# One output tensor, a re-ordered head with nine extra matrix products, and two moves behind the w_out projection, in a streaming hybrid trunk on one core

## The chip, the core and the metric

The kernel runs on one core of a Trainium2 chip. The time is device microseconds (us) of one launch, from its first to its last instruction on the chip with a little around it. Engines are named as in the profile: PE is TensorE's matrix product, PEld its weight load, DVE is VectorE, ACT ScalarE, POOL GpSimd, SP SyncE, which issues most of the DMAs. A "q" behind a name (SPq) is the engine's instruction queue.

## The reference

One layer is computed for 256 new frames (the prompt) and 32 further frames of a running stream (the sample). Both use the same weights, so the kernel treats them as 288 tokens; only histories and states differ. All data are float32, the model width is 2048.

```python
xn   = rmsnorm(x, norm_mix_pre)
proj = xn @ w_in          # -> u_pool 1024 | z 2048 | xBC 2560 | dt 32
y_pool = pool_mixer(u_pool) ; y_ssd, new_h = ssd_mixer(z, xBC, dt, h0)
x    = x + rmsnorm(concat[y_pool, y_ssd] @ w_out, norm_mix_post)
hn   = rmsnorm(x, norm_ffn_pre)
up   = causal_dwconv(hn @ w_up)        # 2 x 5632 columns: gate, value
x    = x + rmsnorm((silu(gate) * value) @ w_down, norm_ffn_post)
# in ssd_mixer, per head:  h_last = decay * h0 + B^T (decay * dt * x)
```

Returned are x for both groups, the last rows of each convolution and pooling input, and the new states `h_last` of prompt and sample.

## The kernel before

**Products.** Activations lie transposed: 128 features on the partitions, 288 tokens along the free axis, so a width of 2048 is 16 K tiles. A float32 product is made of three products of reduced form: weight and activation are each split into a rounded high part (an ACT Copy to `whi`, or to half 0 of `xn`, `hn`, `fa`) and the remainder (a DVE subtraction to `wlo`, or to half 1). `mm3` (L135 to L138) issues high·high (L136), high·low (L137) and low·high (L138) into one PSUM accumulator. So each K tile of weights costs ACT one copy and DVE one subtraction before PE can use it.

**What sets the order.** The code is written against a framework that computes, while the program is built, in which order each engine takes its instructions, from a model of how long each lasts and from priorities. `tc.high_priority(offset=...)` moves instructions ahead, `tc.issue_after(i)` puts an instruction behind `i` on the same engine (nothing waits for it across engines), `tc.keep_in_program_order` fixes an instruction's place. On the chip each engine runs its queue in that fixed order and waits on semaphores. Buffers come from pools and are re-used in turn: five PSUM banks for accumulators (`acc_ps`), three more (`aux`), four each for raw weights, `whi` and `wlo`.

**Stages that the change touches.** The *head* (L245 to L280) computes the first 768 columns of `w_in`: 16 K tiles `k`, six accumulators, 18 products for each `k`. For each `k` it splits `xn` (`split_from`, L99 on ACT and L100 on DVE), splits the weights (L270, L271), and squares the input (`input_squares`, ACT at L233, added on POOL at L234 through two buffers `xsq`); `input_rstd` makes one product `prs` with a constant matrix `mean` (all 1/2048), which sums over partitions, and takes the root. The products `pdt` (L289) follow the head.

The *mixer* (convolution, scan, gates) and the w_out projection come next. At the projection's end lies the *turn* (L744 to L807): `mix_out` squares the last two column tiles into `msq` (L668); the products `psum_m` (L745) close their sum; `state_s` and `state_p` (L689 to L715) form the last two state groups `j` = 3, 2 of four for sample and prompt (`psts`, `pst`, six products), where POOL adds the decayed old state (L714) and SP stores it; `rm` is the root of `psum_m`. Then the residual line on DVE (`residual`, L763 and L764, and the following subtraction, chained by `in_line` in written order) makes `hn` K tile by K tile, while PE multiplies each with 896 columns of `w_up` in seven accumulators (`up1`, weights split at L798 and L799, 21 products for each `k`). Last comes the product `psum_t` (L806) with its root `r2`, written behind the second column tile of the last K tile.

The rest of the FFN is up in tiles of 256 columns and down in two halves. In the *tail* (L943 to L1054) the last two column tiles of down are finished for token block B first (`run_b`), then `y_out` (L963 to L974) scales rows of 128 tokens x 512 columns in `xr` and stores them: four stores of one prompt block, the sample's store from `xr_s` (128 partitions: 4 column blocks x 32 tokens) at L1044, four stores of the other block, after which the kernel ends.

Of the kernel before, what the change touches and what calls it, by code (L numbers as in the profile page):

```python
# [8 lines left out]
F32 = mybir.dt.float32  # L9
F32R = mybir.dt.float32r  # L10
AF = mybir.ActivationFunctionType
ALU = mybir.AluOpType
# [18 lines left out]
NF = D_FF // P  # L31
NXC = CONV // P
NU = D_POOL // P
# [10 lines left out]
def body(  # L44
# [14 lines left out]
    w_up2,  # L59
    w_up,  # L60
    w_down,
    y_prompt,
    y_sample,
    new_pool,
    new_sconv,
    new_ssd_p,
# [16 lines left out]
    def aux(shape, name):  # L83
        return aux_ps.tile(shape, F32, tag="aux", name=name)
# [7 lines left out]
    def split_from(a, src, scale=None):  # L92

        if scale is None:
            act.activation(a[:, 0, :], src, AF.Copy)
            dve.tensor_tensor(a[:, 1, :], src, a[:, 0, :].bitcast(F32), op=ALU.subtract)
        else:
            return (
                act.activation(a[:, 0, :], src, AF.Copy, scale=scale),  # L99
                dve.scalar_tensor_tensor(  # L100
                    a[:, 1, :], src, scale, a[:, 0, :].bitcast(F32), op0=ALU.mult, op1=ALU.subtract
                ),
            )
# [114 lines left out]
    start = ExitStack()  # L218
# [25 lines left out]

    act.dma_start(out=g_mix_pre, in_=g0_in)  # L245
    input_tiles(0, 1)
    first = [acc_ps.tile([P, NT], F32, tag="acc", name="acc") if m < 5 else aux([P, NT], "acc_x") for m in range(6)]
    chunks = ((0, 1), (1, 1)) + tuple((k, 2) for k in range(2, KD, 2))
    x_with = {0: (1, 1), 1: (2, 2), 2: (4, 2), 4: (6, 3), 6: (9, 3), 8: (12, 4)}
    for kb, n in chunks:  # L250
        raw = wpool.tile([P, n, 768], F32, tag="raw", name="raw")
        sp.dma_start(out=raw, in_=w_first[:, kb : kb + n, :])
        if kb in x_with:
            input_tiles(*x_with[kb])
        if kb == 1:
            pool.dma_start(out=wdt, in_=w_dt)
        if kb == 2:
            pool.dma_start(out=par1, in_=par1_in)
            pool.dma_start(out=hp, in_=hp_in)
        if kb == 6:  # L260
            pool.dma_start(out=pc, in_=par2_in[:, :120])
            pool.dma_start(out=pf, in_=par2_in[:, 120:].rearrange("p (r t) -> p r t", r=6))
        for k in range(kb, kb + n):
            a = atile("xn")
            split_from(a, xT[:, k, :], g_mix_pre[:, k : k + 1])
            xn.append(a)
            hi, lo = wtile("hi", 1, 768)[:, 0, :], wtile("lo", 1, 768)[:, 0, :]
            step = 256 if k == 0 else 768
            for c in range(0, 768, step):
                act.activation(hi[:, c : c + step], raw[:, k - kb, c : c + step], AF.Copy)  # L270
                dve.tensor_tensor(  # L271
                    lo[:, c : c + step], raw[:, k - kb, c : c + step], hi[:, c : c + step].bitcast(F32), op=ALU.subtract
                )
# [434 lines left out]
    def state_s(j, x, h, pin=False):  # L708
        st = acc_ps.tile([P, 512], F32, tag="acc", name="psts")
        ins = pe.matmul(st, btok[:, j // 2, 2, :], x[:, 2, :], start=True, stop=True)  # L710
        if pin:
            tc.keep_in_program_order(ins)
        act.activation(x[:, 2, :], st, AF.Copy)
        pool.tensor_tensor(h, h, x[:, 2, :], op=ALU.add)  # L714
        sp.dma_start(out=new_ssd_s[:, 512 * j : 512 * j + 512], in_=h)  # L715

    late_in = {}

# [8 lines left out]
    for grp in ((0, 1), (2,), (3,), (4,), (5,), (6,), (7,)):  # L727
        project(
            wov, [(256 * c, 256) for c in grp], mix, [(8, 8), (16, 8), (0, 8)],
            mix_before(grp[0]), lambda m, p_: mix_out(p_),  # L730
        )
        if 2 <= grp[0] < 4:
            x_h = state_in(grp[0] - 2)
            state_p(grp[0] - 2, *x_h)
            state_s(grp[0] - 2, *x_h)
        elif 4 <= grp[0] < 6:
            late_in[grp[0] - 2] = state_in(grp[0] - 2)
        if grp[0] == 0:
            sp.dma_start(out=xT, in_=x_in)
            act.dma_start(out=new_sconv, in_=sc_stage)  # L740
            act.dma_start(out=new_pool, in_=np_stage)


    for i in range(2):  # L744
        tc.keep_in_program_order(pe.matmul(p_m, mean, last_sq[i], start=False, stop=i == 1))  # L745
# [14 lines left out]
    def in_line(f, *args, **kw):  # L760
        with ExitStack() as order:
            if line:
                order.enter_context(tc.issue_after(line[-1].ins))  # L763
            line.append(f(*args, **kw))  # L764
        return line[-1]
# [6 lines left out]
    for k in range(KD):  # L772
        if k % 2 == 0:
            raw = wpool.tile([P, 2, 896], F32, tag="raw", name="raw")
            with tc.high_priority(offset=ahead[0]):
                sp.dma_start(out=raw, in_=w_up1[:, k : k + 2, :])
        a = atile("hn")
        hi = act.activation(a[:, 0, :], x1[k], AF.Copy, scale=g_ffn_pre[:, k : k + 1])  # L778
        if k + 1 < KD:
            residual(k + 1)  # L780
        lo = in_line(
            dve.scalar_tensor_tensor,
            a[:, 1, :], x1[k], g_ffn_pre[:, k : k + 1], a[:, 0, :].bitcast(F32), op0=ALU.mult, op1=ALU.subtract,
        )
        if k == 0:
            act.activation(xsum, x1[k], AF.Square)
        else:
            q = out_temp()
            act.activation(q, x1[k], AF.Square)
            in_line(dve.tensor_tensor, xsum, xsum, q, op=ALU.add)  # L790
        hn.append(a)
        whi, wlo = wtile("hi", 1, 896)[:, 0, :], wtile("lo", 1, 896)[:, 0, :]
        with ExitStack() as order:
            order.enter_context(tc.high_priority(offset=ahead[0]))
            if k > 3:
                order.enter_context(tc.issue_after(hi.ins))
                order.enter_context(tc.issue_after(lo.ins))
            act.activation(whi, raw[:, k % 2, :], AF.Copy)  # L798
            dve.tensor_tensor(wlo, raw[:, k % 2, :], whi.bitcast(F32), op=ALU.subtract)  # L799
        for m in range(7):  # L800
            c = slice(m * P, (m + 1) * P)
            mm3(up1[m], whi[:, c], wlo[:, c], a, k == 0, k == KD - 1)
            if k == KD - 1 and m == 1:
                r2 = const.tile([P, NT], F32, tag="spread", bufs=3, name="r2")
                with tc.high_priority(offset=1000):
                    tc.keep_in_program_order(pe.matmul(p_t, mean, xsum, start=True, stop=True))  # L806
                    root(r2, p_t)  # L807
# [155 lines left out]
    def y_out(q, b):  # L963

        x = xr[2 * q + b]
        f_ = ft[2 * q + b]
        for o, n, src in (
            ((0, 512, f_),) if q < 3 else ((0, 2 * P, f_[:, : 2 * P]), (2 * P, 2 * P, last[b]))
        ):
            c = slice(o, o + n)  # L970
            ins = dve.scalar_tensor_tensor(x[:, c], src, rf[:, b : b + 1], x[:, c], op0=ALU.mult, op1=ALU.add)  # L971
            if b:
                tc.keep_in_program_order(ins)
        sp.dma_start(out=y_prompt[0][b * P : (b + 1) * P, 512 * q : 512 * (q + 1)], in_=x)  # L974

    n_tok = [0]

# [63 lines left out]
    tc.keep_in_program_order(  # L1041
        dve.scalar_tensor_tensor(xr_s, ft_s, rf[:, 2:3], xr_s, op0=ALU.mult, op1=ALU.add)
    )
    sp.dma_start(out=y_sample[0].rearrange("s (q c) -> q s c", q=4), in_=xr_s)  # L1044
# [11 lines left out]


_OUTS = [
    (1, 256, 2048), (1, 32, 2048), (P, 2, 15, NU), (P, 2, 3, NXC), (P, D_SSD), (P, D_SSD), (P, 2, 2, 2 * NF),
]  # L1060


# [70 lines left out]
```

## Time and profile before

| | |
|---|---|
| time, three runs | 1330.11, 1330.14, 1331.14 us (median 1330.14) |
| profiled execution | 1329.91 us; its span 1328.2 us, so 1.7 us lie around the span |
| mean granted PE clock | 0.997 |
| instructions | 25077, of which PE 10041 |
| busy share of the span | PE 99%, PEld 98%, DVE 67%, ACT 50%, POOL 16% |
| HBM | 236.23 MB read, 11.95 MB written, 187 GB/s |

How to read the rows: a timeline row gives start, duration, engine, line, operation, output<-inputs with their shapes, and in brackets the idle time before it and what ended that. Products overlap in PE's pipeline: each row lasts 0.29 us, though a product starts every 0.13 us or so; the pace is read from the starts. A float32 product that is not split shows as two rows (x2). A row of a window has busy time (and count) for PE, PEld, DVE, ACT and POOL, then the granted clock, the share of the 16 DMA engines in use, and GB/s. A row of the waits view has the engine's waiting tile and line, what released it, then total us, count, longest us.

### The profile page before, as it was taken

How to read it: one execution, taken by the hardware profiler on the slowest of the kernel's cores; microseconds unless marked ns; L12 is line 12 of the kernel's file. 1: busy time of each engine (PE TensorE's matmuls, PEld its weight loads, DVE VectorE, ACT ScalarE, POOL GpSimd, SP SyncE). 2: the span in 40 equal slices, each digit the busy share in tenths (PEclk: the TensorE clock that was granted, in tenths of full speed). 3: DMA queues.
4: the chain of work that ended last, by engine and by line, in shares of the span. 5: the costliest groups of instructions: out<-in, count | busy, mean ns of one | idle time of the engine just before them, and what ended most of it. 6: DMA issues, size and time to landing. Idle time of an engine off the chain costs nothing.

```text
span 1328.2 us, 25077 instructions
## 1 busy us (share of the span) xinstructions
PE 1310.4 (99%) x10041; PEld 1295.1 (98%) x10041; DVE 884.6 (67%) x1460; ACT 666.3 (50%) x1002; POOL 215.0 (16%) x353
## 2 busy tenths in 40 slices
PE   7999999999999999999999999999999999999997
PEld 7999999999999989999999999999999999999996
DVE  8898998779644478977666643345666666664444
ACT  7558777446443455645445443334444444454442
POOL 6221102121211100211111100001111111101110
PEclk9999999999999999999999999999999999999998
DMA  7668884465666445666454454455444544566663
GB/s 287 230 194 255 287 242 160 140 240 206 232 206 207 147 143 195 199 188 185 164 183 162 151 175 161 160 180 177 172 159 164 186 159 159 175 235 175 209 181 93
DMA packets 104008, 249.81 MB, mean 188 GB/s; under 512 B 63748, under 2 KB 69444, under 8 KB 81492
## 3 DMA queue, kind: packets, MB, share of 16 engines
q1 hardware_dynamic: 101972, 243.11, 55.8%
q0 software_dynamic: 1488, 4.92, 1.1%
q8 instruction: 78, 1.28, 0.4%
q14 instruction: 38, 0.31, 0.1%
q10 hardware_dynamic: 432, 0.19, 0.1%
HBM read 236.23 MB, written 11.95 MB: 187 GB/s over the span
## 4 chain that ended last, share of the span: by engine, by line
PE 98%; DVE 1%; DMA 0%; ACT 0%; issue 0%; DVEq 0%; SPq 0%
PE acc L138 31%; PE acc L136 31%; PE acc L137 31%; PE acc_x L138 1%; PE acc_x L137 1%; PE acc_x L136 1%; PE py L467 1%; DVE xr L971 0%; PE run_a L1014 0%; PE low L1012 0%; DMA raw<-in_w_first 0%; PE py L469 0%; PE pst L701 0%; PE run_b L1027 0%; PE pdt L289 0%; DVE mg L764 0%
## 5 line engine op out<-in xcount | busy, mean ns | idle before, releaser
L131 DVE TENSOR_TENSOR wlo<-raw,whi 128x1024 fp32r<-128x1024 f32 (+1 forms) x386 | 464.0, 1203 | 334.7 <-ACT whi L130 332.5
L130 ACT ACTIVATE whi<-raw 128x1024 fp32r<-128x1024 f32 (+1 forms) x386 | 399.6, 1037 | 474.5 <-PE acc L137 382.9
L136 PE MATMUL acc<-hn,whi 128*128 128x288 f32 x1360 | 399.0, 294 | 0.1
L137 PE MATMUL acc<-hn,whi 128*128 128x288 f32 x1360 | 398.1, 293 | 0.0
L138 PE MATMUL acc<-hn,wlo 128*128 128x288 f32 x1360 | 397.7, 293 | 0.0
L136 PEld LDWEIGHTS acc<-hn,whi 128*128 128x128 f32 x1360 | 255.3, 188 | 0.9 <-ACT hn L778 0.9
L137 PEld LDWEIGHTS acc<-hn,whi 128*128 128x128 f32 x1360 | 255.3, 188 | 0.1
L138 PEld LDWEIGHTS acc<-hn,wlo 128*128 128x128 f32 x1360 | 255.2, 188 | 0.0
L136 PE MATMUL acc<-xn,whi 128*128 128x288 f32 x688 | 203.6, 297 | 5.7 <-ACT whi L270 5.7
L137 PE MATMUL acc<-xn,whi 128*128 128x288 f32 x688 | 200.6, 293 | 0.0
L138 PE MATMUL acc<-xn,wlo 128*128 128x288 f32 x688 | 198.6, 298 | 1.3 <-DVE wlo L271 1.3
L136 PE MATMUL acc<-fa,whi 128*128 128x288 f32 x660 | 194.0, 294 | 0.0
L137 PE MATMUL acc<-fa,whi 128*128 128x288 f32 x660 | 193.4, 293 | 0.0
L138 PE MATMUL acc<-fa,wlo 128*128 128x288 f32 x660 | 193.1, 293 | 0.0
L136 PEld LDWEIGHTS acc<-xn,whi 128*128 128x128 f32 x688 | 130.2, 189 | 6.6 <-ACT whi L270 5.7
L137 PEld LDWEIGHTS acc<-xn,whi 128*128 128x128 f32 x688 | 130.1, 189 | 0.2
L138 PEld LDWEIGHTS acc<-xn,wlo 128*128 128x128 f32 x688 | 127.8, 189 | 2.1 <-DVE wlo L271 1.5
L136 PEld LDWEIGHTS acc<-fa,whi 128*128 128x128 f32 x660 | 124.1, 188 | 0.0
L138 PEld LDWEIGHTS acc<-fa,wlo 128*128 128x128 f32 x660 | 123.9, 188 | 0.0
L137 PEld LDWEIGHTS acc<-fa,whi 128*128 128x128 f32 x660 | 123.9, 188 | 0.0
L825 POOL COPY fc_stage<-ebuf 128x4 f32<-128x4 f32 x88 | 27.2, 310 | 501.2 <-DVE ebuf L824 501.2
L831 DVE SCALAR_TENSOR_TENSOR fc<-ebuf,pf,fc 128x290 f32<-128x290 f32 x176 | 90.2, 518 | 2.9 <-ACT fc L829 0.3
(277 smaller groups left out, 1692.0 us busy)
## 6 DMA issues: line engine op xcount, KB each, us to landing
raw<-in_w_up SPq DMA_DIRECT2D x80, 1024.0 KB, 4.8
raw<-in_w_in SPq DMA_DIRECT2D x38, 1024.0 KB, 5.4
raw<-in_w_down SPq DMA_DIRECT2D x32, 1024.0 KB, 4.8
raw<-in_w_out SPq DMA_DIRECT2D x24, 1024.0 KB, 4.9
raw<-in_w_down SPq DMA_DIRECT2D x16, 768.0 KB, 4.3
raw<-in_w_up SPq DMA_DIRECT2D x8, 896.0 KB, 4.6
gb<-g_d SPq DMA_DIRECT2D x8, 832.0 KB, 6.4
raw<-in_w_first SPq DMA_DIRECT2D x7, 768.0 KB, 10.1
```

The source lines that it names most:

```text
L130: act.activation(hi, raw[:, k : k + n, :], AF.Copy)
L131: dve.tensor_tensor(lo, raw[:, k : k + n, :], hi.bitcast(F32), op=ALU.subtract)
L136: pe.matmul(out, wh, a[:, 0, :], start=start, stop=False)
L137: pe.matmul(out, wh, a[:, 1, :], start=False, stop=False)
L138: pe.matmul(out, wl, a[:, 0, :], start=False, stop=stop)
L467: pe.matmul(y[:, 0:256], xw[:, 0, c], m[:, j, 0:256], start=True, stop=False)
L825: pool.tensor_copy(fc_stage[:, :, :, i], e[:, 256:324].rearrange("p (s c) -> p s c", c=34)[:, :, 0:2])
L831: dve.scalar_tensor_tensor(c, e[:, r_ : r_ + 290], pf[:, r_, i : i + 1], c, op0=ALU.mult, op1=ALU.add)
```

## The change

It has four parts.

1. `y_prompt` and `y_sample` become one output `y_rows` of 128 x 9 x 512: the rows of `xr` go to places 0 to 7 of each partition, `xr_s` to place 8, and the host's reshaping puts them back. The stores of `xr` stay 128 x 512 with a longer step between rows; the store of `xr_s` changes from 4 x 32 x 512 to 128 x 512.
2. In the head, nine products `mean` x `mean` of 128 x 128, which nothing reads, stand ahead of the first real one. `xsq` gets four buffers. From `k` = 3 the split of `xn` is issued behind the split of the weights of `k` - 2, the squares behind the weight copy of `k` - 1, and `input_rstd` stands at `k` = 14 rather than 13.
3. The sample's late state addition (`j` = 3, 2) moves from POOL, where it ran right behind the copy of `psts`, to DVE, into the residual line at `k` = 4 and 5; its store on SP follows it.
4. The split of `w_up`'s K tile `k` = 3 is issued behind `hn` of `k` = 3, as that of the later tiles already was.

```diff
@@ outputs and tail
-    y_prompt,
-    y_sample,
+    y_rows,
...
-        sp.dma_start(out=y_prompt[0][b * P : (b + 1) * P, 512 * q : 512 * (q + 1)], in_=x)
+        sp.dma_start(out=y_rows[:, 4 * b + q, :], in_=x)
...
-    sp.dma_start(out=y_sample[0].rearrange("s (q c) -> q s c", q=4), in_=xr_s)
+    sp.dma_start(out=y_rows[:, 8, :], in_=xr_s)
@@ head
-            q = xin.tile([P, NT], F32, tag="xsq", bufs=2, name="xsq")
+            q = xin.tile([P, NT], F32, tag="xsq", bufs=4, name="xsq")
...
+    cut = []
+    idle = aux([P, P], "idle")
+    for i in range(9):
+        tc.keep_in_program_order(pe.matmul(idle, mean, mean, start=True, stop=True))
...
-            split_from(a, xT[:, k, :], g_mix_pre[:, k : k + 1])
+            with ExitStack() as order:
+                for ins in cut[k - 2] if k > 2 else ():
+                    order.enter_context(tc.issue_after(ins.ins))
+                split_from(a, xT[:, k, :], g_mix_pre[:, k : k + 1])
...
+            cut.append((w_hi, w_lo))
             for t in range(k - 1, k) if 0 < k < 9 else range(2 * k - 10, 2 * k - 8) if 8 < k < 13 else ():
-                input_squares(t)
-            if k == 13:
+                with tc.issue_after(cut[k - 1][0].ins):
+                    input_squares(t)
+            if k == 14:
                 input_rstd()
@@ turn
         act.activation(x[:, 2, :], st, AF.Copy)
-        pool.tensor_tensor(h, h, x[:, 2, :], op=ALU.add)
-        sp.dma_start(out=new_ssd_s[:, 512 * j : 512 * j + 512], in_=h)
+
+        def add(eng=pool):
+            ins = eng.tensor_tensor(h, h, x[:, 2, :], op=ALU.add)
+            sp.dma_start(out=new_ssd_s[:, 512 * j : 512 * j + 512], in_=h)
+            return ins
+
+        return add
...
-            state_s(grp[0] - 2, *x_h)
+            state_s(grp[0] - 2, *x_h)()
...
-    state_s(3, *late_in[3], pin=True)
-    state_s(2, *late_in[2], pin=True)
+    late_add = [state_s(j, *late_in[j], pin=True) for j in (3, 2)]
...
+        if 3 < k < 6:
+            in_line(late_add[k - 4], dve)
...
-            if k > 3:
+            if k > 2:
                 order.enter_context(tc.issue_after(hi.ins))
                 order.enter_context(tc.issue_after(lo.ins))
```

The computed order moves with it, in places that no line of the diff names. First, DVE in the head: `wlo` is the remainder of one K tile of weights, `xn` that of one K tile of the input, `g_125` the gain. Before:

```order
L271 TENSOR_TENSOR wlo<-raw,whi 128x768
L284 TENSOR_TENSOR wdt<-wdt,g_125 128x512
L271 TENSOR_TENSOR wlo<-raw,whi 128x768
L100 SCALAR_TENSOR_TENSOR xn<-xT,g_125,xn 128x288 x2
L271 TENSOR_TENSOR wlo<-raw,whi 128x768 x2
L100 SCALAR_TENSOR_TENSOR xn<-xT,g_125,xn 128x288 x6
L271 TENSOR_TENSOR wlo<-raw,whi 128x768 x2
L100 SCALAR_TENSOR_TENSOR xn<-xT,g_125,xn 128x288 x4
L271 TENSOR_TENSOR wlo<-raw,whi 128x768 x8
```

DVE in the head, the same stretch of the changed kernel:

```order
L277 TENSOR_TENSOR wlo<-raw,whi 128x768
L292 TENSOR_TENSOR wdt<-wdt,g_125 128x512
L277 TENSOR_TENSOR wlo<-raw,whi 128x768
L99 SCALAR_TENSOR_TENSOR xn<-xT,g_125,xn 128x288 x2
L277 TENSOR_TENSOR wlo<-raw,whi 128x768 x2
L99 SCALAR_TENSOR_TENSOR xn<-xT,g_125,xn 128x288 x2
L277 TENSOR_TENSOR wlo<-raw,whi 128x768 x2
L99 SCALAR_TENSOR_TENSOR xn<-xT,g_125,xn 128x288 x2
L277 TENSOR_TENSOR wlo<-raw,whi 128x768 x2
L99 SCALAR_TENSOR_TENSOR xn<-xT,g_125,xn 128x288 x2
```

Runs of six and four `xn` have become an alternation of two and two; nothing is taken out or added.

Second, ACT at the turn (the numbers behind names are those of buffers): `msq0` and `msq1` are the squares of the last two column tiles, `mg` their scaled copies, `rm` the root of `psum_m`. Before:

```order
L798 ACTIVATE whi_5887<-raw_5877 128x896
L668 ACTIVATE msq0_3581<-acc_5591 128x288
L670 ACTIVATE mg_5756<-acc_5591,par1_119 128x288
L798 ACTIVATE whi_5920<-raw_5877 128x896
L668 ACTIVATE msq1_3582<-acc_5592 128x288
L670 ACTIVATE mg_5771<-acc_5592,par1_119 128x288
L237 ACTIVATE rm_5798<-psum_m_4205,eps_t_89 128x288
```

ACT at the turn, changed:

```order
L812 ACTIVATE whi_5893<-raw_5883 128x896
L676 ACTIVATE msq0_3591<-acc_5601 128x288
L678 ACTIVATE mg_5766<-acc_5601,par1_119 128x288
L676 ACTIVATE msq1_3592<-acc_5602 128x288
L678 ACTIVATE mg_5781<-acc_5602,par1_119 128x288
L236 ACTIVATE rm_5804<-psum_m_4215,eps_t_89 128x288
```

One weight copy, that of `k` = 3, has left the place between the two squares.

Third, PE at the end of the first up tiles, around `psum_t`. Before:

```order
L136 MATMUL acc<-hn,whi 128x288
L137 MATMUL acc<-hn,whi 128x288
L138 MATMUL acc<-hn,wlo 128x288
L806 MATMUL psum_t<-xsum,mean 128x288
L136 MATMUL acc<-hn,whi 128x288
L137 MATMUL acc<-hn,whi 128x288
L138 MATMUL acc<-hn,wlo 128x288
L136 MATMUL acc_x<-hn,whi 128x288
```

PE at the same place, changed:

```order
L137 MATMUL acc<-hn,wlo 128x288 x3
L137 MATMUL acc_x<-hn,wlo 128x288 x2
L137 MATMUL acc<-hn,wlo 128x288 x2
L820 MATMUL psum_t<-xsum,mean 128x288
L135 MATMUL acc_x<-hn,whi 128x288
L136 MATMUL acc_x<-hn,whi 128x288
L137 MATMUL acc_x<-hn,wlo 128x288
```

`psum_t` has gone from 15 products ahead of the end of the last K tile to directly behind it. The next product there, into `acc_x`, belongs to the next column tile (`w_up2`), and its PSUM bank is the one that `psum_t` used.

More of the change, by code (lines that the diff above doesn't have):

```diff
@@ L269, in body @@
             for c in range(0, 768, step):
-                act.activation(hi[:, c : c + step], raw[:, k - kb, c : c + step], AF.Copy)
-                dve.tensor_tensor(
+                w_hi = act.activation(hi[:, c : c + step], raw[:, k - kb, c : c + step], AF.Copy)
+                w_lo = dve.tensor_tensor(
                     lo[:, c : c + step], raw[:, k - kb, c : c + step], hi[:, c : c + step].bitcast(F32), op=ALU.subtract
                 )
+            cut.append((w_hi, w_lo))
             for t in range(k - 1, k) if 0 < k < 9 else range(2 * k - 10, 2 * k - 8) if 8 < k < 13 else ():
-                input_squares(t)
-            if k == 13:
+                with tc.issue_after(cut[k - 1][0].ins):
+                    input_squares(t)
+            if k == 14:
                 input_rstd()
@@ L1058 @@
 _OUTS = [
-    (1, 256, 2048), (1, 32, 2048), (P, 2, 15, NU), (P, 2, 3, NXC), (P, D_SSD), (P, D_SSD), (P, 2, 2, 2 * NF),
+    (P, 9, 512), (P, 2, 15, NU), (P, 2, 3, NXC), (P, D_SSD), (P, D_SSD), (P, 2, 2, 2 * NF),
 ]
@@ L1119 @@
     r = _run(nc, [arrays], core_ids=[0])
-    y_p, y_s, n_pool, n_sconv, h_p, h_s, n_fconv = (_np.asarray(r.results[0][f"out_{i}"]) for i in range(len(_OUTS)))
+    y, n_pool, n_sconv, h_p, h_s, n_fconv = (_np.asarray(r.results[0][f"out_{i}"]) for i in range(len(_OUTS)))
     def rows(a, s):
@@ L1127, in heads @@
         return _np.ascontiguousarray(a.T).reshape(1, 1, HEADS, 64, P)
+    y_p = _np.ascontiguousarray(y[:, :8].reshape(P, 2, D_MODEL).transpose(1, 0, 2)).reshape(1, NP_, D_MODEL)
+    y_s = _np.ascontiguousarray(y[:, 8].reshape(4, NS, 512).transpose(1, 0, 2)).reshape(1, NS, D_MODEL)
     return (
```

## The prediction

> **What bounds the kernel now.** I read the busy shares first, then the view of PE's waits, then the timeline at the few places where PE waits or crawls, last the chain at the end.
>
> ```profile
> PE 1310.4 (99%) x10041; PEld 1295.1 (98%) x10041; DVE 884.6 (67%) x1460; ACT 666.3 (50%) x1002; POOL 215.0 (16%) x353
> PE acc L136 <- ACT whi L270: 5.7, 1, 5.7
> PE acc L138 <- DVE wlo L271: 1.3, 1, 1.3
> PE psum_f L931 <- ACT fsq L960: 0.8, 1, 0.8
> PE psum_m L745 <- ACT msq L668: 0.7, 1, 0.7
> ```
>
> PE is busy for 99% of the span; the change takes none of its products away and adds nine. What can be won lies where PE waits (two of the four listed waits lie in the head, one at the turn), where its products run at less than their pace, and after its last product. The stretches concerned, in order of time: the start of the head,
>
> ```profile
> 5.71 0.61 PE L136 MATMUL acc<-xn,whi 128*128 128x288 f32 x1 [5.71 <-ACT whi L270]
> 10.87 0.29 PE L137 MATMUL acc<-xn,whi 128*128 128x288 f32 x1
> 5.71:10.87 5.16, 5.16 (x22) 5.16 (x22) 3.95 (x7) 3.69 (x9) 2.49 (x5) 1.00 1.02 376
> 30.25 0.94 PE L138 MATMUL acc<-xn,wlo 128*128 128x288 f32 x5 [1.30 <-DVE wlo L271]
> 48.39 2.08 PE pdt L289 x32
> ```
>
> The row 5.71:10.87 is a window: 22 products in 5.16 us, 0.23 us for each. From 10.87 to 48.39 run the other 266 of the 288, one wait of 1.30 and `prs`; with 0.48 us for `prs` (its row is below) that is (37.52 - 1.30 - 0.48) / 266 = 0.134 us a product, little over half as much. The slow start so costs 5.16 - 22 x 0.134 = 2.2 us. The granted clock in the window's row says 1.00 in spite of it, so I go by the starts.
>
> **The head: nine products and the order.** The changed kernel's first product needs only `mean`, which POOL writes at 0.95 to 1.15. A float32 product of 128 columns, and one of 288, cost:
>
> ```profile
> 0.95 0.20 POOL L183 MEMSET mean<- 128x128 f32 x1
> 112.46 0.22 PE pcb L422 x2
> 40.81 0.48 PE prs L242 x2
> 10.42 1.58 ACT L270 ACTIVATE whi<-raw 128x768 fp32r<-128x768 f32 x2 [1.47 <-DMA raw<-in_w_first]
> 17.98 4.32 DVE L100 SCALAR_TENSOR_TENSOR xn<-xT,g,xn 128x288 fp32r<-128x288 f32 x6
> 25.19 3.53 DVE L100 SCALAR_TENSOR_TENSOR xn<-xT,g,xn 128x288 fp32r<-128x288 f32 x4
> ```
>
> At half pace 0.22 becomes 0.44, so nine last 4.0 us, from about 1.2 to 5.2: just ahead of 5.71, when the first weights are there. They cost nothing unless one takes over (5.71 - 1.2) / 9 = 0.50 us. PE has then been busy for 4.0 us by 5.2; before, full pace came after 5.16 us of work. Bounds for what they bring: nothing, or all of the 2.2. I take all of it, since 4.0 of idle work and 1.2 of real work make the 5.16 by 6.4, and what is still slow there is swallowed by a new wait: K tiles 0 and 1 (36 products, 4.8 us) end by 10.5, but `whi` of `k` = 2 starts at 10.42 behind its DMA and takes half of 1.58, until 11.2. That wait of 0.7 us comes in where PE used to arrive late, so 1.5 remain.
>
> [...]
>
> The stall of 1.30 at 30.25 goes: there `wlo` stood behind runs of six and four `xn` on DVE (4.32 and 3.53 us), which the new order breaks up into twos. ACT and POOL have the squares behind the weight copies now; `prs`, which needs their sum, stands one K tile later, so it is not hurried. Head: 1.5 + 1.3 = 2.8 us. If the idle products bring nothing, 1.3; if the order brings nothing either, 0.
>
> **The turn.**
>
> ```profile
> 475.28 0.95 ACT L798 ACTIVATE whi<-raw 128x896 fp32r<-128x896 f32 x1 [0.63 <-PE acc L137]
> 476.13 0.39 ACT L668 ACTIVATE msq<-acc 128x288 f32<-128x288 f32 x1
> 476.58 0.75 PE L745 MATMUL psum_m<-msq,mean 128*128 128x288 f32 x2 [0.72 <-ACT msq L668]
> 478.88 3.60 PE L701 MATMUL pst<-sx,btok 128*128 128x512 f32 x8
> 478.90 2.71 POOL L714 TENSOR_TENSOR sh<-sh,sx 128x512 f32<-128x512 f32 x2 [20.01 <-ACT sx L713]
> 480.52 1.41 DVE L764 TENSOR_TENSOR mg<-mg,xT 128x288 f32<-128x288 f32 x1
> 482.33 0.46 DVE L764 TENSOR_TENSOR mg<-mg,xT 128x288 f32<-128x288 f32 x1
> 482.55 0.67 PE L136 MATMUL acc<-hn,whi 128*128 128x288 f32 x3
> ```
>
> The weight copy of 0.95 stands between the last product and the last square, and PE waits 0.72 for that square. With the copy gone (its place is behind `hn` of `k` = 3) the square starts when the product is done, and the 0.72 goes nearly whole. Next late is `hn` of `k` = 0: its first addition on DVE took 1.41 us while POOL worked at its two additions, against 0.46 for the same form right after them. Without POOL's additions that is some 0.95 us earlier, while PE has its six state products to do until about 482.4 (3.60 from 478.88), so only 0.1 to 0.2 us show. I take 0.9 for both; bounds 0.6 and 1.1.
>
> **DVE in the up tiles.** DVE gets `wlo` of `k` = 3 later and two additions of 128x512. Nearest rows:
>
> ```profile
> 489.42 1.08 DVE L799 TENSOR_TENSOR wlo<-raw,whi 128x896 fp32r<-128x896 f32 x1
> 497.41 1.08 DVE L799 TENSOR_TENSOR wlo<-raw,whi 128x896 fp32r<-128x896 f32 x1
> 500.06 1.09 DVE L799 TENSOR_TENSOR wlo<-raw,whi 128x896 fp32r<-128x896 f32 x1
> 1317.85 0.74 DVE L1042 SCALAR_TENSOR_TENSOR xr_s<-ft_s,rf,xr_s 128x512 f32<-128x512 f32 x1
> ```
>
> DVE needs 2.65 us for a K tile (from 497.41 to 500.06); PE needs 21 products, 21 x 0.134 = 2.8. So DVE only just keeps pace, and 1.08 + 2 x 0.75 = 2.6 us more must come out of its lead. At 489.42 it subtracts for `k` = 4, which PE reaches four tiles behind 482.55, at about 493.7: a lead of 3 us over the end of the subtraction. `wlo` is used only in the last third of a tile, which gives 1.8 more. I count nothing; bounds 0 and 1.5. Behind the additions, their two stores go to SP between loads of raw weights; an SP issue lasts 0.33 to 0.7 us in the rows of the tail, and the weight loads run ahead by a pool of four buffers: nothing.
>
> **psum_t.**
>
> ```profile
> 524.92 0.65 PE L806 MATMUL psum_t<-xsum,mean 128*128 128x288 f32 x2
> 525.61 0.50 ACT L237 ACTIVATE r<-psum_t,eps_t 128x288 f32<-128x288 f32 x1 [0.35 <-PE psum_t L806]
> ```
>
> Before, 15 products cover the root between `psum_t` and the first product into `acc_x`, which takes over its PSUM bank. Changed, that product is the very next one and may only write when ACT has read the bank: 525.61 + 0.50 - 524.92 = 1.19 us after `psum_t` begins, where it could have begun after 0.48. A new wait of 0.7 us. All later products are queued behind it on PE, so it reaches the end whole. Lower bound 0.5 (the root's own reading), upper 1.0 (a way from PE to ACT and back 0.3 longer than here).
>
> **The tail.**
>
> ```profile
> 1316.59 0.33 SPq L974 DMA_DIRECT2D out<-xr  x1
> 1318.62 0.70 SPq L1044 DMA_DIRECT2D out<-xr_s  x1
> 1320.68 1.67 SPq L974 DMA_DIRECT2D out<-xr  x1
> 1322.92 1.23 SPq L974 DMA_DIRECT2D out<-xr  x1
> DMA to landing us min/median/max: 2.0/2.1/2.1
> DMA to landing us min/median/max: 4.2/4.8/5.3
> 1317.00:1318.00 1.00, 0.57 (x6) 0.38 (x4) 0.97 (x4) 0.04 (x1) 0.00 (x0) 1.00 1.02 383
> 1321.00:1322.00 1.00, 0.00 (x0) 0.00 (x0) 1.00 (x3) 0.00 (x0) 0.00 (x0) 0.76 0.20 43
> 1326.00:1327.00 1.00, 0.00 (x0) 0.00 (x0) 0.00 (x0) 0.00 (x0) 0.00 (x0) 0.50 0.17 64
> 1320.65 1.45 DVE xr L971 x3
> ```
>
> The two landing rows are the four stores ahead of the sample's (2.1 us) and the four behind it (4.8). Before the sample's store the DMA engines are all busy at 383 GB/s; behind it a fifth of them works at 43 GB/s, and still so at 1326. So the one store of 4 x 32 x 512 keeps a few engines for some 8 us, the stores behind it wait for these few, and even SP's issues stretch from 0.33 to 1.67 and 1.23. The last store is issued at 1322.92 and lands 4.3 later, at 1327.2. Stored like its neighbours, the sample lands in 2.1 us, the last store is issued when DVE is done (1320.65 + 1.45 = 1322.1) and lands at 1324.2. That is 3.0 us earlier; the chain before it is the same. Bounds: 0 (if the engines are held by something else) and 3.2.
>
> [...]
>
> **The sum.** -2.8 (head) - 0.9 (turn) + 0.7 (psum_t) - 3.0 (tail) = -6.0 us. The profiled execution took 1329.91, so the changed one 1323.9; the median of the runs shown lies 0.23 above the profiled one, so I predict 1324.1.
>
> **The rivals.** *The idle products do not bring full pace earlier.* For it: nothing in this trace shows work of this kind setting the pace. Against: the pace changes once, in the middle of a K tile, after steady work. Then the head gives 1.3 and the time is 1325.6.
>
> *The tail's slow stores are not the sample's doing*, but of the end of the kernel as such. For it: only one such store exists, so the trace shows one order of events. Against: 0.33 becomes 1.67 right behind it. Then the tail gives nothing: 1327.1, if the rest holds.
>
> *DVE falls behind in the up tiles.* Its surplus is 0.15 us a tile and 2.6 us are loaded on it. PE then waits at `hn` or `wlo` from `k` = 4 on, up to 1.5 us: 1325.6. The lead read above speaks against it.
>
> *Slower: the idle products hold up the head.* They stand ahead of the first real product in PE's fixed order, and no row shows such a product on a PE that has done nothing yet. From 0.50 us each they delay the head; 0.7 of the delay is taken up by the wait for `k` = 2, and the gain of 6.0 is gone at 0.50 + 6.7 / 9 = 1.24 us each. At 1.4 us the nine end at 1.2 + 12.6 = 13.8, the first real product comes 8.1 later than 5.71, and the kernel takes 1324.1 + 8.1 - 0.7 = 1331.5. The 0.22 row, and 0.61 for the first slow product of 288 columns, speak against it.
>
> That the change does not do what it says at the store can be left out: its new form, 128 rows from 128 partitions, is that of the `xr` stores that land in 2.1 us.
>
> **How the numbers follow.** Forecast 0.73; no earlier pace 0.10; tail not from the store 0.08; DVE behind 0.06; held head 0.03. The range goes down to 1322.6: 0.2 more at the turn, 0.4 in the head if its small gaps close too, 0.2 in the tail, 0.2 less at psum_t, and 0.5 for a median that need not lie as far from the profiled execution as here. It goes up to 1326.2, which holds both cases at 1325.6 with 0.3 more at psum_t and 0.3 less at the turn; left out are the tail's case and the held head, 0.11, and what I cannot name. A measurement of this kernel can tell 0.2%, 2.7 us, from no change. Faster than 1327.5 are the forecast, the two cases at 1325.6 and one half of the tail's case, 0.93; the other half, in which a second term fails too, makes the 0.04 within 0.2%; slower has the held head's 0.03.
>
> **What would show it.** In the changed profile: products every 0.13 us from the first real one on and a wait of about 0.7 for `whi` of `k` = 2; no wait for `wlo` in the head, `pdt` at about 45.6; PE's wait at `psum_m` gone and one of 0.7 behind `psum_t`; stores in the tail that land in 2.1 us, the last one issued within 0.4 us of DVE's end. The prediction is wrong if the first real product starts later than 5.71, if the slow pace goes on beyond 8 us, if new PE waits appear between `k` = 4 and 8 of the up tiles, or if the last store lands over 3 us after its issue.

## The result and the profile after

| | before | changed |
|---|---|---|
| time, median of five runs | 1330.12 us (1330.04 to 1331.14) | 1324.51 us (1324.36 to 1325.44) |
| span of the profiled execution | 1328.2 us | 1322.8 us |
| PE busy, products | 1310.4 us, 10041 | 1312.1 us, 10059 |

The ratio is 0.9956, with a 95% interval of 0.9943 to 0.9969: faster by 5.6 us (0.4%), where 6.0 were forecast (1324.1). The span of the profiled execution is 5.4 us shorter; the nine added products show as 18 rows. Where the 5.4 us come in is read best by setting the starts of the same products in both traces side by side. First PE's waits in the changed kernel (waiting tile and line, releaser, total us, count, longest):

```profile
PE acc L135 <- ACT whi L276: 2.0, 2, 1.7
PE idle L249 <- POOL mean L182: 1.2, 1, 1.2
PE psum_f L945 <- ACT fsq L974: 0.8, 1, 0.8
PE acc_x L135 <- ACT r L236: 0.6, 1, 0.6
```

The wait for `wlo` in the head and the one of `psum_m` are gone; two new ones are there, for the weights of K tile 2 (1.7 us) and behind `psum_t` (0.6 us). Now the head's timeline, the load in the chain that PE waits for there, and the chain's `pdt`:

```profile
1.21 3.77 PE L249 MATMUL idle<-mean 128*128 128x128 f32 x18 [1.21 <-POOL mean L182]
5.34 0.40 PE L135 MATMUL acc<-xn,whi 128*128 128x288 f32 x1 [0.36 <-ACT whi L276]
5.58 0.29 PE L136 MATMUL acc<-xn,whi 128*128 128x288 f32 x1
5.71 0.29 PE L135 MATMUL acc<-xn,whi 128*128 128x288 f32 x1
3.14 8.02 DMA raw<-in_w_first
12.08 0.40 PE L135 MATMUL acc<-xn,whi 128*128 128x288 f32 x1 [1.68 <-ACT whi L276]
46.23 2.08 PE pdt L297 x32
```

The idle products end before the weights come, and from 5.58 on a product starts every 0.13 us. PE is 2.6 us ahead of its old self when K tile 1 ends, and gives 1.9 of them back at 12.08, where it waits for a load issued at 3.14. `pdt` starts 48.39 - 46.23 = 2.16 us earlier. At the turn and at `psum_t` (rows of the chain, of DVE, PE and ACT; the last row is of the kernel before, its counterpart of the row above it):

```profile
473.38 0.75 PE psum_m L758 x2
477.18 0.46 DVE L776 TENSOR_TENSOR mg<-mg,xT 128x288 f32<-128x288 f32 x1
478.72 0.83 PE L135 MATMUL acc<-hn,whi 128*128 128x288 f32 x2
523.73 0.65 PE L820 MATMUL psum_t<-xsum,mean 128*128 128x288 f32 x2
524.41 0.50 ACT L236 ACTIVATE r<-psum_t,eps_t 128x288 f32<-128x288 f32 x1 [0.35 <-PE psum_t L820]
524.97 0.40 PE L135 MATMUL acc_x<-hn,whi 128*128 128x288 f32 x1 [0.59 <-ACT r L236]
527.39 0.29 PE L136 MATMUL acc_x<-hn,whi 128*128 128x288 f32 x1
```

The products `psum_m` that close the sum are 476.58 - 473.38 = 3.20 us ahead, the first up product 482.55 - 478.72 = 3.83 (3.53 from the second on), the first product into `acc_x` behind `psum_t` 527.39 - 524.97 = 2.42 (2.32 from the second on). In the tail, SP's issues, the landing of the last four stores, and the chain's end:

```profile
1316.31 0.33 SPq L1058 DMA_DIRECT2D out<-xr_s  x1
1317.71 0.33 SPq L988 DMA_DIRECT2D out<-xr  x1
1319.82 0.33 SPq L988 DMA_DIRECT2D out<-xr  x1
DMA to landing us min/median/max: 2.0/2.1/2.1
1318.34 1.45 DVE xr L985 x3
```

Every issue lasts 0.33 to 0.34 us and every store lands in 2.0 to 2.1. DVE's last rows are 1320.65 - 1318.34 = 2.31 us ahead, the end 5.4: the tail gave 3.1.

The account, worked out from these starts (and, inside a stage, from the starts of the same products):

| place | forecast | measured | what it was |
|---|---|---|---|
| head, to `pdt` | 2.8 | 2.16 | pace +2.6, K tile 2 -1.9, `wlo` stall +1.45 |
| mixer | 0 | 0.33 | one gap ahead of the first `py` (130.7 to 131.8 in the trace of before); E4, with the mixer as before, is 0.30 shorter there too, so it is not shown to be the change's |
| turn | 0.9 | 1.04 | `psum_m` 0.71; the up products, from the second on, another 0.33 |
| first up tiles | 0 | -0.34 | no wait; a slower pace between 495 and 520 |
| `psum_t` | -0.7 | -0.87 | the wait for the root |
| tail | 3.0 | 3.1 | the sample's store |
| sum | 6.0 | 5.4 | |

### The profile page after: what moved, and what is told of

The parts are those of the page before. It is cut to its first block, busy times and chain, and to the rows that moved or that the text cites. A ratio compares the mean times of both kernels' runs of the same rounds, so it can differ in the third digit from the quotient of the medians.

```text
span 1322.8 us, 25112 instructions
## 1 busy us (share of the span) xinstructions
PE 1312.1 (99%) x10059; PEld 1296.8 (98%) x10059; DVE 883.8 (67%) x1462; ACT 666.0 (50%) x1002; POOL 219.9 (17%) x351
## 4 chain that ended last, share of the span: by engine, by line
PE 98%; DMA 1%; DVE 0%; SPq 0%; ACT 0%; DVEq 0%; issue 0%
PE acc L135 31%; PE acc L137 31%; PE acc L136 31%; PE acc_x L135 1%; PE acc_x L137 1%; PE py L475 1%; PE acc_x L136 1%; DMA raw<-in_w_first 1%; PE pst L709 1%; DVE xr L985 0%; PE run_a L1028 0%; PE low L1026 0%; PE py L477 0%; PE psts L718 0%; PE run_b L1041 0%; PE pdt L297 0%
## 5 line engine op out<-in xcount | busy, mean ns | idle before, releaser
L135 PE MATMUL acc<-hn,whi 128*128 128x288 f32 x1360 | 394.3, 294 | 0.0
L136 PE MATMUL acc<-hn,whi 128*128 128x288 f32 x1360 | 393.4, 293 | 0.0
L137 PE MATMUL acc<-hn,wlo 128*128 128x288 f32 x1360 | 392.5, 293 | 0.0
L137 PE MATMUL acc<-xn,wlo 128*128 128x288 f32 x688 | 194.9, 295 | 0.0
```

The costliest lines, as they stand in the source:

```text
L135: pe.matmul(out, wh, a[:, 0, :], start=start, stop=False)
L136: pe.matmul(out, wh, a[:, 1, :], start=False, stop=False)
L137: pe.matmul(out, wl, a[:, 0, :], start=False, stop=stop)
```

## The experiments

Twelve kernels were run, each beside the kernel before on the same chip. Medians of that kernel lay at 1330.1 to 1330.8 in the different sets, so single medians are compared to about 0.5 us only, and effects below that are read from the starts in the traces, against the profile of the changed kernel.

### The nine idle products

Taken away (E1):

```diff
-    idle = aux([P, P], "idle")
-    for i in range(9):
-        tc.keep_in_program_order(pe.matmul(idle, mean, mean, start=True, stop=True))
```

> The changed kernel without the nine idle products; all else as changed. Theory A (what bounds the head's start is the transfer of K tile 2's weights): the first real products are slow again, some 22 at 0.23 us, so PE reaches K tile 2 at about 12.3 instead of 10.4; its weights were ready at 12.1 in the changed kernel, so the wait of 1.7 us goes and only 0.2 to 0.5 us is lost: about 1324.9. Theory B (the prediction's sum, where the idle products bring 1.5 us): 1326.0. Theory C (idle products do not set the pace): pace and time as in the changed kernel, 1324.5.

1324.92 us, ratio 0.9958 (0.9941 to 0.9975). The window of the first real products, then of the next, the chain's `pdt`, and ACT's split of K tile 2:

```profile
5.56:10.60 5.04, 5.04 (x23) 5.04 (x24) 3.58 (x7) 3.35 (x8) 2.27 (x4) 1.00 0.99 361
10.60:11.60 1.00, 1.00 (x9) 1.00 (x9) 0.08 (x1) 0.96 (x2) 0.00 (x0) 1.00 1.04 397
46.32 2.08 PE pdt L294 x32
10.64 1.58 ACT L273 ACTIVATE whi<-raw 128x768 fp32r<-128x768 f32 x2 [1.26 <-DMA raw<-in_w_first]
```

The slow pace is back (the first products start 0.24 us apart up to 9.8, then 0.13), yet `pdt` starts only 0.09 us later than with the idle products, and no wait for K tile 2 is left. Theory A held for this pair of executions, and the prediction's 1.5 us for these products did not. The load came earlier here, though: `whi` of K tile 2 starts at 10.64, in the changed kernel at 11.18. With the load at the same time the idle products bring some 0.6 us, as worked out in the next section.

Doubled (E2, `range(18)`):

> The changed kernel with 18 idle products instead of nine. Theory A: nine more at full pace, 0.22 us each, end near 7.0, so the first real product comes 1.6 us later than 5.34; the wait for K tile 2 (1.7 us) shrinks to about 0.1 and the time stays: 1324.5, at most 0.3 more. Rival (what stands ahead of the first real product is paid in full): 1.6 us more, 1326.1.

1324.81 us, 0.9955 (0.9940 to 0.9970).

```profile
1.21 6.78 PE L249 MATMUL idle<-mean 128*128 128x128 f32 x36 [1.21 <-POOL mean L182]
7.75 0.38 PE L135 MATMUL acc<-xn,whi 128*128 128x288 f32 x1
46.40 2.08 PE pdt L297 x32
```

The 18 end at 7.99 and not near 7.0, since full pace came later than expected: the eight rows that lie in 4.0 to 5.3 last 1.91 us together, so still some 0.2 us from start to start. The first real product comes 2.4 us later and `pdt` 0.17: most of a delay of 2.4 us is hidden by the same wait that hides the gain. (Here too the load came early, `whi` at 10.63; measured from it, 0.7 us of the delay are paid.)

### The head's order

The old order with the idle products kept (E9):

```diff
-                for ins in cut[k - 2] if k > 2 else ():
-                    order.enter_context(tc.issue_after(ins.ins))
...
-                with tc.issue_after(cut[k - 1][0].ins):
-                    input_squares(t)
-            if k == 14:
+                input_squares(t)
+            if k == 13:
```

and `xsq` with two buffers.

> The changed kernel with the head in its old order (xn not behind the earlier split, squares free, two xsq buffers, prs at K tile 13), the nine idle products kept. Theory A (the head's gain is the order's, by the stall of 1.3 to 1.45 us at wlo of K tile 8): the stall comes back, 1.3 to 1.5 us more, about 1325.9. Theory B (the idle products bring most of it): up to 0.5 more, 1325.0.

1327.78 us, 0.9980 (0.9971 to 0.9990): 3.3 us more than the changed kernel, over twice what theory A said.

```profile
22.55 0.40 PE L135 MATMUL acc<-xn,whi 128*128 128x288 f32 x1 [1.11 <-ACT whi L274]
30.54 0.93 PE L137 MATMUL acc<-xn,wlo 128*128 128x288 f32 x5 [1.36 <-DVE wlo L275]
48.69 2.08 PE pdt L294 x32
```

`pdt` is at 48.69, against 48.39 in the kernel before: on the old order the idle products gain nothing. PE, now early, meets a wait for `whi` at 22.55 that its slow start hid in the trace of before (0.48 of it shows in E4, where the load came later), and the stall at `wlo` as before. (The other 0.9 us were lost at the first `py` of the mixer, where PE sat idle for 0.66 us without a releaser that the profile shows; why is open.)

These starts of `pdt` mix the head's order with the time at which K tile 2's weights happen to arrive. The kernel before itself shows it, in E4 (described below), whose head is that of before:

```profile
11.18 1.58 ACT L270 ACTIVATE whi<-raw 128x768 fp32r<-128x768 f32 x2 [1.51 <-DMA raw<-in_w_first]
49.15 2.08 PE pdt L289 x32
```

So the head is better measured from the start of `whi` of K tile 2 to that of `pdt`:

| order, idle products | executions | `whi` of K tile 2 | `pdt` | from one to the other |
|---|---|---|---|---|
| old, none | before, E4 | 10.42, 11.18 | 48.39, 49.15 | 37.97, 37.97 |
| old, nine | E9 | 10.71 | 48.69 | 37.98 |
| new, none | E1 | 10.64 | 46.32 | 35.68 |
| new, nine | changed, E3, E6, E7, E8, E10 | 9.96 to 11.18 | 45.01 to 46.23 | 35.02 to 35.05 |
| new, eighteen | E2 | 10.63 | 46.40 | 35.77 |

With nine idle products, and in the old order with or without them, the distance is the same to 0.03 us: the head's end follows the arrival of that load, or of the loads that come with it. At the same arrival the order is worth 2.3 us without idle products and 2.9 with them. The idle products bring nothing on the old order and 0.6 on the new one at E1's arrival (more with an earlier load, less with a later one, if PE without them comes no sooner than in E1). E9 undoes four things at once (place of the `xn` split, place of the squares, `xsq` buffers, place of `prs`); which of them carries the order's gain was not separated.

### The sample's store

First, the same pattern as before, but into the one output (E3):

```diff
-    sp.dma_start(out=y_rows[:, 8, :], in_=xr_s)
+    sp.dma_start(out=y_rows[:, 8, :].rearrange("(q s) c -> q s c", q=4), in_=xr_s)
```

> The changed kernel, but the sample's store goes to its place in the one output as 4 x 32 x 512 instead of 128 x 512: same source, same destination bytes. Theory A (the pattern's four-fold slowest dimension keeps the store on few DMA engines): the tail is that of before, later stores land 4 to 5 us after issue, SP's issues stretch to over 1 us, about 3.1 us more: 1327.6. Rival (the one output tensor, or its row step, is what helped): landing 2.0 to 2.1, 1324.5.

1324.01 us, 0.9951 (0.9936 to 0.9966). This told nothing about the store: in the one output the four blocks lie at an even step, and the built kernel has the pattern folded to 128 x 512, so that it is the changed kernel instruction for instruction (1296 DMA packets in the tail in both, the sample's store landing in 2.0 us in both). It is a second run of that kernel, 0.5 us faster than the first, with K tile 2's `whi` 0.43 us earlier in the profiled execution.

Second, the kernel before with its own sample output and four stores (E4):

```diff
-    sp.dma_start(out=y_sample[0].rearrange("s (q c) -> q s c", q=4), in_=xr_s)
+    for q in range(4):
+        sp.dma_start(out=y_sample[0][:, 512 * q : 512 * (q + 1)], in_=xr_s[NS * q : NS * q + NS, :])
```

> The kernel before, with the sample's store as four stores of 32 x 512, one for each column block, into its own output tensor. Theory A: each of the four can use many DMA engines; they cost three more issues of 0.33 us on SP, which end before the next store is due, so the tail's 3 us come in without any one-tensor output: about 1327.2 (0.9977 of before). Rival (it is the sample's separate tensor, or the store's place in the queue, that holds the later stores up): 1330.1.

1327.93 us, 0.9980 (0.9971 to 0.9989). Landing of the four stores behind it, the last issue, and the sample's four stores (KB each, median us to landing):

```profile
DMA to landing us min/median/max: 2.1/2.4/2.5
1322.58 0.33 SPq L974 DMA_DIRECT2D out<-xr  x1
out<-xr_s SPq DMA_DIRECT2D x4, 64.0 KB, 1.7
```

2.4 us instead of 4.8, and SP's issue back at 0.33: the same bytes to the same place, without the one 4 x 32 x 512 pattern, bring most of the tail's gain without any one-tensor output. From DVE's last rows to the end it is 5.2 us, against 7.55 before and 4.46 in the changed kernel, so 2.35 of the 3.1.

Third, in the changed kernel the store undone, and at the turn the place of K tile 3's split (E10): an output `y_sample` with the old store, and `k > 3` for `k > 2`.

> The changed kernel with two of its parts undone, which lie far apart and are read at their own places: the sample goes to an output of its own again as one 4 x 32 x 512 store, and the split of up's K tile 3 stands ahead of hn again. Theory A: behind the sample's store the others land 4 to 5 us after issue and the time from PE's last product to the end grows by 3.0 us; psum_m waits 0.7 us for the second square again; together 3.7 us, about 1328.2. Rival for the tail (its gain was the one tensor's): it does so as well, so this run does not tell them apart, the four-store run does. Rival for the turn (the copy's place was covered by the state products): no wait at psum_m, 1327.5.

1328.42 us, 0.9988 (0.9979 to 0.9997), 3.9 us more than the changed kernel.

```profile
473.97 0.75 PE L759 MATMUL psum_m<-msq,mean 128*128 128x288 f32 x2 [0.72 <-ACT msq L677]
1321.39 1.20 SPq L989 DMA_DIRECT2D out<-xr  x1
DMA to landing us min/median/max: 4.1/4.8/5.3
```

Both effects return at their places and in their size: 0.72 us at `psum_m`, and in the tail 3.0 us (PE's last products are 0.76 us later than in the changed kernel, the end 3.8).

### The turn and psum_t

The late additions back on POOL (E8): `state_s(j, *late_in[j], pin=True)()` at once, and no `late_add` in the line.

> The changed kernel with the sample's late state additions back on POOL right behind their copies; the split of K tile 3 stays behind hn. Theory A (POOL's two additions of 1.35 us slow DVE's first residual addition from 0.46 to 1.41 us, and hn of K tile 0 is what the up tiles wait for): the up tiles start 0.4 to 0.6 us later, of which DVE's lighter load gives nothing back: 1325.0. Rival (the gain at the turn was all of the weight copy's): the DVE addition takes 0.46 as well, or is hidden by the state products; 1324.5.

1324.50 us, 0.9957 (0.9943 to 0.9972).

```profile
475.01 2.71 POOL L724 TENSOR_TENSOR sh<-sh,sx 128x512 f32<-128x512 f32 x2 [19.30 <-ACT sx L721]
476.63 1.41 DVE L777 TENSOR_TENSOR mg<-mg,xT 128x288 f32<-128x288 f32 x1
478.44 0.46 DVE L777 TENSOR_TENSOR mg<-mg,xT 128x288 f32<-128x288 f32 x1
```

With POOL's additions DVE's addition beside them lasts 1.41 us again, and the up tiles start 0.33 us later. But 0.30 of it comes back by the end of the up tiles (a shorter wait behind `psum_t`, 0.3 instead of 0.6, and a little pace), where theory A expected nothing back. It held for the mechanism; over the whole kernel this part of the change is worth nothing that can be measured.

`psum_t` ahead of 15 products (E6):

```diff
+                if k == KD - 1 and m > 1:
+                    order.enter_context(tc.issue_after(pt_ins.ins))
                 mm3(up1[m], whi[:, c], wlo[:, c], a, k == 0, k == KD - 1)
```

> The changed kernel with the last K tile's products for column tiles 2 to 6 issued behind psum_t, so that 15 products cover its root. Theory A: the wait of acc_x for the root (0.6 us and the idle pipeline with it, 0.87 us in the comparison of the two traces) goes and nothing else comes late: 1323.7. Rival (xsum or another operand is late at the earlier place, which is why it was moved): PE waits at psum_t and the time stays within 0.2 of 1324.5.

1323.06 us, 0.9945 (0.9930 to 0.9960). No wait is left at `acc_x` or at `psum_t`. The products behind it are 2.12 us ahead of the changed kernel's, those before it 1.23: 0.89 us at this place, as theory A said. (The 1.23 lie in the head, which is the same code: its weights came earlier in this execution.)

The order in threes as well (E7): from K tile 4 of the first up tiles each product of `mm3` is issued behind the one before it.

> The changed kernel with the products of the first up tiles from K tile 4 on kept in the order high-high, high-low, low-high for each column tile, as they mostly stood before, and psum_t in its old place by that. Theory A (the order itself sets PE's pace: 0.1312 us a product in threes, 0.1329 when the same kind runs over all seven accumulators): 252 products gain 0.0017 each, 0.4 us, beside the 0.87 of psum_t: 1323.3, pace in the stretch 495 to 520 back to 0.1312. Rival 1 (the pace is lost to something else, DVE or DMA): pace stays at 0.1329, 1323.7. Rival 2 (a strict order makes PE wait for wlo, which DVE brings late now): waits for wlo at L813, 1324.5 or more.

1322.61 us, 0.9943 (0.9926 to 0.9959), the fastest of all. Windows of 495 to 520 us, in which PE never waits: the kernel before, the changed one, this one.

```profile
495.00:520.00 25.00, 25.00 (x192) 25.00 (x192) 24.29 (x46) 15.91 (x27) 0.00 (x0) 1.00 0.48 157
495.00:520.00 25.00, 25.00 (x190) 25.00 (x189) 24.41 (x44) 15.71 (x26) 0.00 (x0) 1.00 0.47 154
495.00:520.00 25.00, 25.00 (x193) 25.00 (x192) 23.70 (x42) 15.38 (x26) 0.00 (x0) 1.00 0.49 160
```

190 products against 192 and 193: the starts lie 0.1329 us apart on average in the changed order (all high-high products of the seven accumulators, then the others), 0.1312 in threes. Against the changed kernel this run gains 0.39 us in the stretch, and 0.90 at `psum_t`; another 0.87 lie in the head, by the earlier load. Theory A held; `wlo` made no wait.

### What K tile 2 waits for

The parameter loads moved behind the fourth square (E5), their first readers behind K tile 9.

> The changed kernel with the five parameter loads that POOL issues at 3.7 to 6.5 us (some 0.7 MB: wdt, par1, hp, pc, pf) issued behind the fourth square instead, and their first readers on DVE and ACT moved behind K tile 9. Theory A (K tile 2 waits for DMA bandwidth, which is full at 350 to 400 GB/s from 4 us on): 0.7 MB less in front of it, up to 1.8 us; the wait of 1.7 us before K tile 2 falls to 0.3 or less, pdt comes 1.4 to 1.7 us earlier, time about 1323.0. Rival (the latency of that load's own queue, not bandwidth): the wait stays at 1.7 and the time at 1324.5.

1323.40 us, 0.9948 (0.9933 to 0.9963), which looks like a gain. But `whi` of K tile 2, released by its load, started here (first row) between its starts in two runs with the parameter loads where they were (E6, then the changed kernel):

```profile
10.50 1.58 ACT L277 ACTIVATE whi<-raw 128x768 fp32r<-128x768 f32 x2 [0.88 <-DMA raw<-in_w_first]
9.96 1.58 ACT L276 ACTIVATE whi<-raw 128x768 fp32r<-128x768 f32 x2 [1.32 <-DMA raw<-in_w_first]
11.18 1.58 ACT L276 ACTIVATE whi<-raw 128x768 fp32r<-128x768 f32 x2 [1.29 <-DMA raw<-in_w_first]
```

The gain lies within the spread of that load's arrival. The expected 1.4 us did not come; theory A is not borne out in this form.

K tiles 2 and 3 loaded one by one, with E7's order (E11):

> The changed kernel with the first up tiles' products in threes and psum_t early (as in the run that did this alone, 1322.6), and with K tiles 2 and 3 of the head loaded one by one instead of as a pair, so that the next pair waits for a raw buffer. Theory A (K tile 2 is late because its transfer is one of two tiles and shares full DMA engines with the loads queued behind it): its weights are there by 10.4, the wait of 0.5 to 1.7 us goes, 1321.6. Rival (its arrival does not depend on that): 1322.6, the wait stays.

1323.33 us, 0.9950 (0.9935 to 0.9965): not better than E7 alone.

```profile
9.16 0.85 ACT L280 ACTIVATE whi<-raw 128x768 fp32r<-128x768 f32 x1 [0.38 <-DMA raw<-in_w_first]
15.66 1.58 ACT L280 ACTIVATE whi<-raw 128x768 fp32r<-128x768 f32 x2 [1.55 <-DMA raw<-in_w_first]
16.56 0.40 PE L136 MATMUL acc<-xn,whi 128*128 128x288 f32 x1 [0.68 <-ACT whi L280]
46.11 2.08 PE pdt L301 x32
```

K tile 2 is indeed there earlier, at 9.16, but the next pair comes only at 15.66, and PE waits for that instead. And the same without the idle products (E12):

> The run before without the nine idle products. Theory A (the idle products' 2 us were hidden by K tile 2's late weights and are not hidden once these are early): 1.5 to 2.1 us slower than that run, 1323.4. Rival (they bring nothing in any case): equal to it within 0.3.

1323.27 us, 0.9950 (0.9933 to 0.9967): equal, `pdt` at 45.74. Theory A fell; the rival held.

So the head, once its order is right, is bound by its loads. What stays open is which transfers share the way of K tile 2's; fewer bytes from POOL (E5) and smaller pieces (E11) were each tried alone, not together.

## Why the prediction was right, and where it was not

**The time** was 1324.51 for 1324.1, inside the range, and the two large terms were of the right size. In the head that is luck: two errors cancel, as follows.

**Tail, right in size and cause.** 3.1 us for 3.0. E4 and E10 show that it is the single 4 x 32 x 512 store that holds the later ones up, not the separate tensor. The rival without a gain in the tail is out. In E4 the sample's stores of 32 rows land in 1.7 us at the median, and those behind them in 2.4. How many DMA engines a store takes was not counted in any run; the shares agree with few for the old one. While the sample's store is the only one whose data move, the share is 0.44 and 0.29, at 57 and 16 GB/s, in the kernel before (1320.00 to 1320.25 and on to 1320.50), and 1.04 and 1.01, at 393 and 385 GB/s, in the changed one (1317.25 to 1317.50 and on to 1317.75). Why the old pattern does that was not shown: no run varied its outermost dimension by itself.

**Head, right sum, wrong split.** The forecast was 2.8 us: 1.5 for the idle products and 1.3 for the order. In the two profiled executions the sum was 2.16, but there the load of K tile 2 came 0.76 us later than before (`whi` at 11.18 against 10.42); at the same arrival it is 2.9, of which the order brings 2.3 and the idle products 0.6. So the step "I take all of it ... so 1.5 remain" failed. Full pace did come earlier with the idle products: at 4.14 and near 7.4 us into the span in E6 and E10 with nine of them, near 9.8 and 10.8 in E1 and the kernel before without, which rules out the rival that they do not bring it. The 2.6 us so won by 9.44 in the changed kernel are given back, wholly or for the most part, at the next thing that PE waits for (E1, E2, E9, E12). The wait for K tile 2 was put at 0.7 us from one row of before, 10.42; that load lands at a different time in each execution (`whi` at 9.96 to 11.18), and the wait was between 1.7 and less than 0.3 us (in E7). And the order's 1.3 was too small: it counted the one stall at `wlo` that the trace of before shows, while with an early PE the old order has a second wait, hidden before (E9). A slip beside this: the 22 of the window 5.71:10.87 count the product that starts at its end; with 21 the slow start costs 2.3 us rather than 2.2.

Nor does full pace come at one time. Windows of E6 (idle products at first slow, then fast) and of E10 (real products slow, then fast):

```profile
1.20:4.14 2.94, 2.93 (x13) 2.94 (x14) 0.62 (x2) 2.02 (x3) 2.90 (x26) 1.00 0.76 192
4.14:4.70 0.56, 0.56 (x6) 0.53 (x5) 0.27 (x1) 0.00 (x0) 0.56 (x2) 1.00 0.98 319
5.07:7.38 2.31, 2.31 (x12) 2.31 (x12) 1.82 (x5) 2.31 (x6) 1.53 (x4) 1.00 0.92 281
7.38:9.38 2.00, 2.00 (x16) 2.00 (x16) 0.80 (x2) 0.71 (x3) 1.24 (x1) 1.00 0.98 381
```

The change from slow to fast lies at 4.14 in the one and near 7.4 in the other, 2.9 and 6.2 us after the first idle product, with the same instructions. What sets the time was not shown. The 8 us that the prediction gives as the limit of the slow pace was the author's estimate, which no run shows. In E10 the late change cost nothing, since PE waited 0.81 us for K tile 2 all the same.

**Turn, right.** 1.04 us for 0.9; the 0.72 of `psum_m` by the copy's place (E10), 0.33 by POOL's additions (E8), which I had put at 0.1 to 0.2.

**First up tiles, missed.** I looked for a wait of DVE there and, rightly, counted none. What was lost, 0.34 us, is pace: the edit moved the planned order of the products, and PE is 1.3% slower in it (E7). Which part of the edit moved it is open: with the additions back on POOL (E8), and with K tile 3's split ahead of `hn` (E10), the products still start 0.1327 us apart. I had read the new order only at `psum_t`.

**psum_t, right.** 0.87 for 0.7; E6 takes it back.

**Slower rival.** The idle products last 0.42 us each (3.77 / 9), under the 0.50 from which they would delay the first real product; and E2 shows that even a delay of 2.4 us would have cost 0.2 to 0.7.

## What to carry to other kernels

A faster start is worth only as much as the next wait lets through: before counting a pace gain, list what the engine will meet early, with the spread of its arrival over several executions, not one row. When such an arrival varies, measure a stage from the arrival and not from the start of the span. Here one store whose outermost dimension was 4 held up every store behind it (4.8 us at the median from issue to landing, not 2.1); giving such a store the shape of its neighbours took no more than a split into four. When an edit changes an engine's load, read the new order of the other engines over the whole stage: here two moves on PE that no line of the edit names cost 1.2 of 6.6 us, and putting them back gives the fastest version, 1322.61 us.

## What the runs showed of the hardware that was not expected

The order of equal products changed PE's pace between 495 and 520 us: 0.1312 us a product in threes on one accumulator (E7; the first two of the three with the same weight tile), 0.1329 when neighbours go to different accumulators (the changed kernel), without any wait in either. Why was not tried. The granted clock of the profile read 1.00 in windows in which the products ran at little over half pace (in the window 5.07:7.38 of E10 they start 0.24 us apart, at full pace 0.13). And one load of the head, issued at 3.13 to 3.15 us in each execution, came in at times 1.2 us apart (`whi` of K tile 2 at 9.96 to 11.18).
